# Computing the gating half v with seven products of block sums instead of eight of blocks

## The chip, the cores and the metric

One NeuronCore of a Trainium2 chip runs the whole program. Five engines work side by side, each through its own queue of instructions in a fixed order: TensorE (PE, matrix products, its weight loads listed as PEld), VectorE (DVE), ScalarE (ACT), GpSimd (POOL) and SyncE (SP, which here only issues DMAs). An instruction whose inputs are not there holds up all that is queued behind it on its engine. The metric is the device time of one execution in microseconds (us): less is better.

## The reference, cut to what matters

Two layers of a diffusion backbone over 512 latent tokens of 1024 features. Layer 0 is a neighbourhood attention followed by a squared-ReLU MLP, layer 1 a spatial gating unit followed by another MLP. The change is in the spatial gating unit, whose input h is 512 x 1024 and whose weight w_in is 1024 x 6144:

```
z = gelu(h @ w_in + b_in)
u, v = split(z, 2)
v = layer_norm(v, ln_g, ln_b)
s = einsum('gpq,bnqgc->bnpgc', w_s, v) + b_s
return (u * s) @ w_o
```

So v, before its norm, is gelu of a 512 x 1024 by 1024 x 3072 product and a bias. All is float32.

## The kernel before, in words

**Products.** A float32 value is split into two parts, hi (rounded to the TensorE format float32r) and lo (the rest), and a product is three matmuls, hi*hi, hi*lo and lo*hi (`products`, L178). Activations are split once per stage: `h_hi`/`h_lo` are eight tiles of 128 features x 512 tokens. Weights are split as they arrive.

**The weight stream.** All weights lie in one array in the order of their use (`SECTIONS`, L39), cut into units of 128 x 1536. `Weights.load` fetches a unit to a tile `raw` (768 KB, two buffers) through SP's queue. `Weights.upto` splits it in four pieces of 128 x 384: ACT casts `whi<-raw` (L80), DVE subtracts `wlo<-raw,whi` (L81). `get` asks for the pieces of one product and splits one unit ahead of them; three pairs whi/wlo, four after the attention, take turns.

**The stage of v** (L601 to L618). For each of six column blocks of 512 and each of four token blocks of 128, 24 matmuls of 512 columns (8 feature chunks by 3) fill one bank: 6 x 4 x 24 = 576 matmuls. Then DVE adds the bias (L616), ACT applies gelu (L617) and DVE takes the statistics of the later norm (L618). Behind it come the products of u (`u0`, ...), the norm of v and the products with w_s.

**The stage ahead of it** is the first MLP (`mlp`, L598): in two halves, 16 hidden blocks (24 matmuls each) and then 8 output blocks (48 matmuls each, L512 adds them to the residual stream `xall`). Into it 56 calls of `ada_block` are woven (L273): each loads 512 KB of the modulation weights to the one buffer `adaraw` (L276, SP) and reduces them on DVE (L277), so a load waits for the reduction before it. After the last output block `normed` (L494) makes the next `h_hi`/`h_lo`, token half by token half.

**The order.** Instructions are put into each engine's queue by a scheduler that works before the launch from its own estimates of times; the queues are then fixed. `tc.issue_after` binds an `ada_block` behind the hidden block that it follows, no more.

Of the kernel before, what the change touches and what calls it, by code (L numbers as in the profile page):

```python
# [10 lines left out]
F32 = mybir.dt.float32  # L11
F32R = mybir.dt.float32r
AF = mybir.ActivationFunctionType
ALU = mybir.AluOpType
# [3 lines left out]
P = 128  # L18
D = 1024
KC = D // P  # L20
T = 512
# [6 lines left out]
UNIT = 1536  # L28
# [9 lines left out]
# The weight stream: sections of pieces in the order of their use, (name, pieces, columns of a piece).  # L38
# [8 lines left out]

class Weights:
    """Streams of stationary or moving weight pieces, split into two float32r parts on arrival."""

    def __init__(self, nc, raw_pool, pool, wall, ahead=2):
        self.nc, self.raw_pool, self.pool, self.ahead, self.wall = nc, raw_pool, pool, ahead, wall
        self.first, self.width = {}, {}
        c = 0
        for key, n, w in SECTIONS:
            self.first[key], self.width[key] = c, w
            c += n * w
        self.tiles = {}
        self.raw = {}
        self.loaded = self.done = 0  # L60
        self.more, self.parts = None, 4

    def load(self, unit):
        while self.loaded <= min(unit, self.wall.shape[0] - 1):
            raw = self.raw_pool.tile([P, UNIT], F32, tag="raw", bufs=2, name="raw")
            self.nc.sync.dma_start(out=raw, in_=self.wall[self.loaded])
            self.raw[self.loaded] = raw
            self.loaded += 1

    def upto(self, unit):  # L70
        nc = self.nc
        while self.done <= min(unit, self.wall.shape[0] - 1):
            self.load(self.done)
            raw = self.raw.pop(self.done)
            pool = self.more if self.more is not None and self.done % 4 == 3 else self.pool
            hi = pool.tile([P, UNIT], F32R, tag="whi", name="whi")
            lo = pool.tile([P, UNIT], F32R, tag="wlo", name="wlo")
            for c in range(0, UNIT, UNIT // self.parts):
                cs = slice(c, c + UNIT // self.parts)
                nc.scalar.copy(out=hi[:, cs], in_=raw[:, cs])  # L80
                nc.vector.tensor_tensor(out=lo[:, cs], in0=raw[:, cs], in1=hi[:, cs], op=ALU.subtract)  # L81
            self.tiles[self.done] = (hi, lo)
            self.done += 1

    def get(self, key, i):
        w = self.width[key]
        u, c = divmod(self.first[key] + i * w, UNIT)
        assert c + w <= UNIT
        self.upto(u + self.ahead - 1)
        hi, lo = self.tiles[u]  # L90
        return hi[:, c:c + w], lo[:, c:c + w]
# [3 lines left out]
def backbone_kernel(ctx: ExitStack, tc: tile.TileContext, x0T, xT, cols, ada0, ada1, qknorm, bias_t,  # L95
                    wall, wsT, bs, binv, lngb, out):
    nc = tc.nc
# [10 lines left out]
    def mm():  # L108
        return bank("mm", 3)
# [16 lines left out]
    def mcol(l, v, kc):  # L126
        i = (l * 6 + v) * KC + kc
        return mod[:, i:i + 1]
# [5 lines left out]
    h_hi = [hp.tile([P, T], F32R, tag=f"hh{k}", name=f"hh{k}") for k in range(KC)]  # L134
    h_lo = [hp.tile([P, T], F32R, tag=f"hl{k}", name=f"hl{k}") for k in range(KC)]

    class Norm:
        """Reciprocal RMS over the feature axis (partitions and chunks), on every partition."""
# [39 lines left out]
    def products(o, terms, start, stop):  # L178
        n = len(terms) * 3
        i = 0  # L180
        for (ah, al), (bh, bl) in terms:
            for a, b in ((ah, bh), (ah, bl), (al, bh)):
                pe.matmul(o, lhsT=a, rhs=b, start=start and i == 0, stop=stop and i == n - 1)  # L183
                i += 1

# [297 lines left out]
    W.more = ctx.enter_context(tc.tile_pool(name="wb", bufs=1, reuse_waits="tile"))  # L483
# [15 lines left out]
    def normed(nm, A, shift):  # L499
        """What turns a finished half of the residual stream into the next sub-layer's input."""  # L500
        def go(c0, c1):
            r = nm.finish(c0, c1)
            modulated(xp, x, r, c0, c1, A, shift, h_hi, h_lo)
# [43 lines left out]
    nm = Norm(xp)  # L547
    residual("o", NPAIR, oh, ol, lambda m: mcol(0, 2, m), first=4, tail=3, nm=nm,
             then=normed(nm, A2[0], lambda k: mcol(0, 3, k)))
    ap_stack.close()  # L550

# [45 lines left out]
    nm = Norm(xp)  # L597
    mlp(0, "a", 24, 80, nm, normed(nm, A1[1], lambda k: mcol(1, 0, k)), None)  # L598
    cb_pool.close()

# [1 line left out]
    with tc.tile_pool(name="sg", bufs=1, reuse_waits="tile") as sp:  # L602
# [4 lines left out]
        for b in range(6):  # L607
            w = [W.get("v", b * KC + k) for k in range(KC)]
            bb = sp.tile([P, 512], F32, tag="bc", bufs=2, name="bc")
            act.dma_start(out=bb, in_=binv[b].partition_broadcast(P))  # L610
            for n in range(4):
                ns = slice(n * P, (n + 1) * P)
                o = mm()
                products(o, [((h_hi[k][:, ns], h_lo[k][:, ns]), w[k]) for k in range(KC)], True, True)
                vs = v[:, n, b * 512:(b + 1) * 512]
                vec.tensor_tensor(out=vs, in0=o, in1=bb, op=ALU.add)  # L616
                act.activation(out=vs, in_=vs, func=AF.Gelu)  # L617
                vec.bn_stats(out=stats[n][:, b], in_=vs)  # L618
# [19 lines left out]
        nm = Norm(xp)  # L638
        for part in range(4):
            gh, gl = [], []  # L640
            for i in range(6):
# [13 lines left out]
                for n in range(4):  # L655
# [15 lines left out]
                     then=normed(nm, A2[1], lambda k: mcol(1, 3, k)) if fin else None)  # L671

    mlp(1, "b", 80, 80, None, None, out)

# [102 lines left out]
```

## Time and profile before

| what | value |
|---|---|
| device time, median of 3 runs | 1563.95 us (1559.7 to 1568.19) |
| span of the profiled execution, first to last instruction (the only time shown of it) | 1560.2 us |
| PE busy | 1524.9 us, 98% of the span |
| DVE busy | 930.1 us, 60% |
| ACT busy | 664.3 us, 43% |
| stage of v on PE | 782.4 to 914.7 us |
| first MLP's second half, hidden blocks done on PE | 686.8 us |

Busy times of PE overlap, since matmuls are pipelined: the pitch from one start to the next is what a matmul costs. The same holds in part for DVE, where a run of instructions on independent data starts the next before the last is wholly written; the pitch is again read from starts. "Idle before" and the name behind an arrow tell how long an engine waited and for what.

### The profile page before, as it was taken

The page shows a single profiled execution, that of the slowest core. Times are in us where ns is not written, and L with a number is a line of the kernel's source. Part 1 is how long each engine was busy: PE and PEld are TensorE (multiplying, and loading weights), DVE is VectorE, ACT ScalarE, POOL GpSimd, SP SyncE. Part 2 cuts the span into 40 slices and gives each one's busy share as a digit, 9 for nine tenths or more (in the row PEclk, how much of TensorE's full clock was granted, in tenths as well). Part 3 has the DMA queues.
Part 4 walks back from the last instruction along what each step waited for, and adds up shares of the span by engine and source line. Part 5 has one row for each costly group of instructions (what it writes and reads, how often), then busy time and mean ns, then how long its engine had stood idle before and what let it go on. Part 6 is the DMA issues. An engine that isn't in the chain of part 4 may idle for free.

```text
span 1560.2 us, 21105 instructions
## 1 busy us (share of the span) xinstructions
PE 1524.9 (98%) x7780; PEld 1287.6 (83%) x7780; DVE 930.1 (60%) x1938; ACT 664.3 (43%) x1577; POOL 148.8 (10%) x177
## 2 busy tenths in 40 slices
PE   8899999999999999999999999999999999999999
PEld 2798888887898888878988887888889988888888
DVE  5778777777776555765575468644446743334431
ACT  2566666676544322442353256423234542224320
POOL 0522222212200000000100013100001000000000
PEclk9999999999999999999999999999999999999999
DMA  9265555535146555655243225322321432223230
GB/s 354 95 171 174 164 163 167 167 113 167 62 142 211 193 193 180 202 199 179 95 128 131 91 96 176 125 92 97 106 95 41 135 109 87 96 101 102 97 112 28
DMA packets 60311, 212.06 MB, mean 136 GB/s; under 512 B 7984, under 2 KB 16816, under 8 KB 58672
## 3 DMA queue, kind: packets, MB, share of 16 engines
q1 hardware_dynamic: 48688, 200.57, 39.2%
q10 hardware_dynamic: 11520, 10.15, 2.1%
q8 instruction: 61, 1.00, 0.3%
q14 instruction: 42, 0.34, 0.1%
HBM read 193.91 MB, written 2.10 MB: 126 GB/s over the span
## 4 chain that ended last, share of the span: by engine, by line
PE 59%; DMA 8%; DVE 4%; issue 2%; ACT 1%; ACTq 0%; DVEq 0%
PE ps_mm L183 29%; PE ps_t L183 19%; PE ps_o L183 9%; DMA adaraw<-ada 8%; DVE adaraw L277 1%; PE ps_s L656 1%; DVE wlo L81 1%; DVE nt L172 1%; DVE hl L174 0%; DVE xall L512 0%; DMA raw<-wall 0%; PE ps_s L156 0%; ACT v L632 0%; DVE acc L151 0%; ACT whi L80 0%
## 5 line engine op out<-in xcount | busy, mean ns | idle before, releaser
L80 ACT CAST whi<-raw 128x384 fp32r<-128x384 f32 x620 | 278.5, 510 | 355.9 <-PE ps_mm L183 141.5
L81 DVE TENSOR_TENSOR wlo<-raw,whi 128x384 fp32r<-128x384 f32 x620 | 330.6, 581 | 144.8 <-ACT whi L80 144.6
L277 DVE CUSTOM_DVE_ANT_0 adaraw<-adaraw,cb 128x1024 f32<-128x1024 f32 x80 | 99.4, 1242 | 106.6 <-DMA adaraw<-ada 106.1
L183 PE MATMUL ps_mm<-hh,wlo 128*128 128x512 f32 (+1 forms) x416 | 154.2, 371 | 0.6 <-DVE wlo L81 0.6
L183 PE MATMUL ps_mm<-hh,whi 128*128 128x512 f32 (+1 forms) x416 | 154.4, 371 | 0.0
L183 PE MATMUL ps_mm<-hl,whi 128*128 128x512 f32 (+1 forms) x416 | 154.0, 370 | 0.0
L183 PE MATMUL ps_mm<-whi,hh 128*128 128x384 f32 (+1 forms) x352 | 124.7, 356 | 5.1 <-DVE vl L332 2.9
L183 PE MATMUL ps_mm<-wlo,hh 128*128 128x384 f32 (+1 forms) x352 | 124.8, 355 | 1.9 <-DVE wlo L81 1.9
L183 PE MATMUL ps_mm<-mh,whi 128*128 128x512 f32 (+1 forms) x336 | 122.0, 363 | 3.2 <-ACT mh L566 3.2
L183 PE MATMUL ps_mm<-whi,hl 128*128 128x384 f32 (+1 forms) x352 | 124.1, 354 | 0.0
L183 PE MATMUL ps_mm<-ml,whi 128*128 128x512 f32 (+1 forms) x336 | 122.1, 363 | 0.0
L183 PE MATMUL ps_mm<-mh,wlo 128*128 128x512 f32 (+1 forms) x336 | 121.6, 362 | 0.0
L183 PE MATMUL ps_t<-hh,whi 128*128 128x512 f32 (+1 forms) x280 | 104.5, 373 | 0.0
L183 PE MATMUL ps_t<-hl,whi 128*128 128x512 f32 (+1 forms) x280 | 104.3, 372 | 0.0
L183 PE MATMUL ps_t<-hh,wlo 128*128 128x512 f32 (+1 forms) x280 | 104.0, 371 | 0.0
L183 PEld LDWEIGHTS ps_mm<-hh,wlo 128*128 128x128 f32 x416 | 78.5, 189 | 13.8 <-DVE wlo L81 0.8
L183 PEld LDWEIGHTS ps_mm<-hh,whi 128*128 128x128 f32 x416 | 78.5, 189 | 12.6
L183 PEld LDWEIGHTS ps_mm<-hl,whi 128*128 128x128 f32 x416 | 78.6, 189 | 12.5
L566 ACT CAST mh<-relu 128x512 fp32r<-128x512 f32 x64 | 39.7, 621 | 99.0 <-DVE relu L563 99.0
L183 PEld LDWEIGHTS ps_mm<-mh,whi 128*128 128x128 f32 x336 | 64.2, 191 | 13.1 <-ACT mh L566 3.6
L183 PEld LDWEIGHTS ps_mm<-whi,hh 128*128 128x128 f32 x352 | 66.6, 189 | 10.2 <-DVE vl L332 3.2
L183 PEld LDWEIGHTS ps_mm<-wlo,hh 128*128 128x128 f32 x352 | 66.8, 190 | 7.5 <-DVE wlo L81 2.8
(204 smaller groups left out, 3322.5 us busy)
## 6 DMA issues: line engine op xcount, KB each, us to landing
raw<-wall SPq DMA_DIRECT2D x155, 768.0 KB, 4.4
adaraw<-ada SPq DMA_DIRECT2D x80, 512.0 KB, 3.9
bt<-bias_t SPq DMA_DIRECT2D x16, 512.0 KB, 3.6
aw<-ada SPq DMA_DIRECT2D x7, 1024.0 KB, 10.8
q<-th SPq DMA_DIRECT2D x32, 128.0 KB, 2.4
q<-tl SPq DMA_DIRECT2D x32, 128.0 KB, 2.3
x<-x0T SPq DMA_DIRECT2D x3, 1024.0 KB, 11.3
bc<-lngb ACTq DMA_DIRECT2D x12, 256.0 KB, 3.3
```

The source lines that it names most:

```text
L80: nc.scalar.copy(out=hi[:, cs], in_=raw[:, cs])
L81: nc.vector.tensor_tensor(out=lo[:, cs], in0=raw[:, cs], in1=hi[:, cs], op=ALU.subtract)
L172: vec.scalar_tensor_tensor(out=t, in0=xk, scalar=A[:, k:k + 1], in1=r, op0=ALU.mult, op1=ALU.mult)
L183: pe.matmul(o, lhsT=a, rhs=b, start=start and i == 0, stop=stop and i == n - 1)
L277: vec.tensor_tensor_reduce(out=a, in0=a, in1=cb, scale=1.0, scalar=0.0, op0=ALU.mult, op1=ALU.add, accum_out=mod[:, idx:idx + 1])
L566: act.copy(out=a, in_=r)
L656: pe.matmul(s[:, n * P:(n + 1) * P], lhsT=v[:, n, g * P:(g + 1) * P], rhs=ws, start=True, stop=True)
```

## The change: what it does

The product for v is taken in three rounds, one for each 1024 columns of the weight. In a round h is cut into quarters (two halves of the features, B11 and B21 for the first 256 tokens, B12 and B22 for the last), the weight into four blocks W00, W10, W01, W11 of 512 features x 512 columns. Instead of eight block products the kernel forms seven (Winograd's form of Strassen's scheme): n1 = W00 with B11, n2 = W10 with B21, and five with sums T1 to T4 of quarters of h or with sums of weight blocks. Each is 4 feature chunks x 2 token blocks x 3 = 24 matmuls of 512 columns; three rounds have 3 x 7 x 24 = 504.

The sums of h are made once, ahead of the rounds: DVE adds hi and lo of each quarter again (4 instructions of 128 x 1024), forms T1, T3, T2 and T4 (4) and their lo parts (4), ACT casts their hi parts. The sums of weight blocks are made in every round on DVE from loads of the blocks: W01+W11 (kept in `sum0`, `sum1`, one for each half block), that plus W00, W00+W01 (in a raw tile), and the kept sum plus W10. The seven weight operands are then split like other weights. Bank X collects n1, n6, n7 and n4 without being cleared between, Z collects n5 and n3; after each product DVE takes what the bank holds so far into v, adding or subtracting, and gelu and statistics follow when a part is complete.

For this the weight stream is now loaded in tiles of 128 x 1024 (512 KB, three buffers) and split in pieces of 128 x 512 in the whole program; the eight tiles of `h_hi` and `h_lo` are one tile each; and the fourth pair of whi/wlo is given up during the stage of v and opened anew after it.

```diff
+PRODUCTS = (("n1", "B11"), ("n2", "B21"), ("n5", "T1"), ("n6", "T2"), ("n7", "T3"), ("n3", "B22"), ("n4", "T4"))
+def summands(blocks):
+    w00, w01, w10, w11 = blocks
+    return ((False, (w00,)), (False, (w10,)), (None, (w01, w11)), (True, (w00,)), (False, (w00, w01)),
+            (True, (w10,)), (False, (w11,)))
...
+            slot, go_on, what = self.stretches[self.loaded]
+            if go_on:
+                raw = self.sums[slot]
+            elif slot is None:
+                raw = self.raw_pool.tile([P, RAW], F32, tag="raw", bufs=3, name="raw")
+            else:
+                raw = self.sums[slot] = self.sum_pool.tile([P, RAW], F32, tag=f"sum{slot}", name=f"sum{slot}")
+            if not go_on:
+                self.nc.sync.dma_start(out=raw, in_=self.dram(what[0], RAW))
+                what = what[1:]
+            for c in what:
+                t = self.raw_pool.tile([P, RAW], F32, tag="raw", bufs=3, name="raw")
+                self.nc.sync.dma_start(out=t, in_=self.dram(c, RAW))
+                self.nc.vector.tensor_tensor(out=raw, in0=raw, in1=t, op=ALU.add)
...
+    def split(self, src, hi, lo):
+        self.nc.scalar.copy(out=hi, in_=src)
+        self.nc.vector.tensor_tensor(out=lo, in0=src, in1=hi, op=ALU.subtract)
...
-        for b in range(6):
-            w = [W.get("v", b * KC + k) for k in range(KC)]
...
-                products(o, [((h_hi[k][:, ns], h_lo[k][:, ns]), w[k]) for k in range(KC)], True, True)
...
+            for q, (ks, ts) in quarter.items():
+                f[q] = vp.tile([P, HK, HT], F32, tag="f" + q, name="f" + q)
+                vec.tensor_tensor(out=f[q], in0=hh_all[:, ks, ts], in1=hl_all[:, ks, ts], op=ALU.add)
+            def operand(name, a, b, reverse, into):
+                if reverse:
+                    vec.scalar_tensor_tensor(out=into, in0=a, scalar=-1.0, in1=b, op0=ALU.mult, op1=ALU.subtract)
+                else:
+                    vec.tensor_tensor(out=into, in0=a, in1=b, op=ALU.subtract)
...
+                act.copy(out=hi, in_=into)
+                vec.tensor_tensor(out=lo, in0=into, in1=hi, op=ALU.subtract)
...
+            for u in range(3):
...
+                into = {"n1": X, "n2": Y, "n5": Z, "n6": X, "n7": X, "n3": Z, "n4": X}
+                for j, (name, q) in enumerate(PRODUCTS):
+                    hi, lo = ops[q]
+                    o = into[name]
+                    for k in range(HK):
+                        w = W.get("v", (u * 7 + j) * HK + k)
+                        for i in range(2):
+                            ts = slice(i * P, (i + 1) * P)
+                            products(o[i], [((hi[:, k, ts], lo[:, k, ts]), w)],
...
+                        if name == "n6":
+                            plus(at_(1, 0), bb[:, 0])
+                        if name == "n7":
+                            minus(at_(1, 1), at_(1, 1))
+                            done = [(1, 1)]
+                        if name == "n3":
+                            plus(at_(1, 0), at_(1, 0))
+                            done = [(1, 0)]
```

DVE's queue where the stage of v begins, in the kernel before (the numbers behind hl and hh are the feature chunks' tiles):

```order
L159 RECIPROCAL rstd<-rstd 128x256
L81 TENSOR_TENSOR wlo<-raw,whi 128x384
L172 SCALAR_TENSOR_TENSOR nt<-xall,A_1_83,rstd 128x256 x2
L616 TENSOR_TENSOR v<-ps_mm,bc 128x512
L174 SCALAR_TENSOR_TENSOR hl_95<-nt,mod,hh_87 128x256
L170 TENSOR_TENSOR hl_96<-nt,hh_88 128x256
```

The same place in the changed kernel, from the last of the four sums of hi and lo on, which stand right behind the second token half's norm (fB are the quarters, sum_7827 is `sum0`):

```order
L683 TENSOR_TENSOR fB_7760<-hh,hl 128x1024
L690 TENSOR_TENSOR fB_7754<-fB_7754,fB_7756 128x1024
L115 TENSOR_TENSOR sum_7827<-sum_7827,raw 128x1024
L690 TENSOR_TENSOR fB_7756<-fB_7760,fB_7756 128x1024
L694 TENSOR_TENSOR T1l<-fB_7754,T1h 128x1024
L688 SCALAR_TENSOR_TENSOR fB_7760<-fB_7754,fB_7760 128x1024
L694 TENSOR_TENSOR T3l<-fB_7756,T3h 128x1024
L688 SCALAR_TENSOR_TENSOR fB_7758<-fB_7760,fB_7758 128x1024
L694 TENSOR_TENSOR T2l<-fB_7760,T2h 128x1024
L126 TENSOR_TENSOR wlo<-sum_7827,whi 128x512
L694 TENSOR_TENSOR T4l<-fB_7758,T4h 128x1024
```

The sums of h now stand as one block behind the norm, and the first split that n5 needs (`wlo<-sum_7827`) stands behind nearly all of it.

DVE's queue in the middle of the stage, before (raw_7998, raw_8124 and raw_8136 are units of the weight stream):

```order
L616 TENSOR_TENSOR v_7817<-ps_mm_8068,bc_8010 128x512
L81 TENSOR_TENSOR wlo_8001<-raw_7998,whi_8000 128x384 x4
L618 BN_STATS st2_7820<-v_7817 128x6
L81 TENSOR_TENSOR wlo_8127<-raw_8124,whi_8126 128x384 x4
L616 TENSOR_TENSOR v_7817<-ps_t_8096,bc_8010 128x512
```

And in the changed kernel's second round, where W00+W01 is formed (raw_8246 and raw_8277 are the two halves of W00, raw_8248 and raw_8279 those of W01, raw_8306 and raw_8315 those of W10):

```order
L115 TENSOR_TENSOR raw_8246<-raw_8246,raw_8248 128x1024
L126 TENSOR_TENSOR wlo_8241<-sum1_8177,whi_8240 128x512 x2
L126 TENSOR_TENSOR wlo_8241<-raw_8246,whi_8240 128x512
L728 SCALAR_TENSOR_TENSOR v_7744<-ps_s_8122,bb_8115 128x512
L728 SCALAR_TENSOR_TENSOR v_7744<-ps_s_8123,bb_8115 128x512
L126 TENSOR_TENSOR wlo_8274<-raw_8246,whi_8273 128x512
L731 TENSOR_TENSOR v_7744<-ps_mm_8118,bb_8115 128x512
L115 TENSOR_TENSOR raw_8277<-raw_8277,raw_8279 128x1024
L731 TENSOR_TENSOR v_7744<-ps_mm_8119,bb_8115 128x512
L126 TENSOR_TENSOR wlo_8274<-raw_8277,whi_8273 128x512 x2
L115 TENSOR_TENSOR sum0_8166<-sum0_8166,raw_8306 128x1024
L115 TENSOR_TENSOR sum1_8177<-sum1_8177,raw_8315 128x1024
```

Sums of freshly loaded tiles now stand between the splits and the steps that empty the banks, and an addition stands one row behind the last split of the tile three loads earlier.

DVE's queue in the first MLP, the last two hidden blocks of the second half, before:

```order
L563 SCALAR_TENSOR_TENSOR relu<-ps_t,relu 128x512
L567 TENSOR_TENSOR ml_7039<-relu,mh_7038 128x512
L81 TENSOR_TENSOR wlo<-raw,whi 128x384 x4
L277 ISA adaraw,mod<-adaraw,cb 128x1024
L277 ISA mod 128x1
L563 SCALAR_TENSOR_TENSOR relu<-ps_o,relu 128x512
L567 TENSOR_TENSOR ml_7083<-relu,mh_7082 128x512
```

And in the changed kernel:

```order
L628 SCALAR_TENSOR_TENSOR relu<-ps_t,relu 128x512
L336 ISA adaraw,mod<-adaraw,cb 128x1024
L336 ISA mod 128x1
L632 TENSOR_TENSOR ml_6974<-relu,mh_6973 128x512
L126 TENSOR_TENSOR wlo<-raw,whi 128x512 x3
L336 ISA adaraw,mod<-adaraw,cb 128x1024
L336 ISA mod 128x1
L628 SCALAR_TENSOR_TENSOR relu<-ps_o,relu 128x512
L632 TENSOR_TENSOR ml_7018<-relu,mh_7017 128x512
```

The change's text leaves this place alone, but the scheduler gave it another order: two reductions stand between the last two blocks where one stood. Counted over the queue, 56 of the program's 80 reductions stand ahead of the first of these 16 blocks in either kernel; ahead of the last block it was 71, and is 74. In the first half 37 stood ahead of the last hidden block, and 38 do now.

## Rows read from the trace of the kernel before

**Rows 1.** The page's first part: busy time, share and instructions of each engine.

```profile
PE 1524.9 (98%) x7780; PEld 1287.6 (83%) x7780; DVE 930.1 (60%) x1938; ACT 664.3 (43%) x1577; POOL 148.8 (10%) x177
```

**Rows 2.** Stretches: length, busy of PE, PEld, DVE, ACT, POOL, PEclk, DMA, GB/s.

```profile
782.40:914.70 132.30, 131.30 (x581) 108.45 (x580) 73.76 (x136) 50.60 (x105) 2.84 (x4) 1.00 0.34 112
```

**Rows 3.** PE in order of time, the stage of v: start, duration, instruction.

```profile
782.37 0.40 PE L183 MATMUL ps_mm<-whi,hh 128*128 128x512 f32 x1
...
786.50 0.70 PE L156 MATMUL ps_s<-acc,ones 128*128 128x256 f32 x2 [1.00 <-DVE acc L151]
...
914.47 0.39 PE L183 MATMUL ps_mm<-whi,hl 128*128 128x512 f32 x1
914.69 0.39 PE L183 MATMUL ps_mm<-hh,whi 128*128 128x512 f32 x1
```

**Rows 4.** DVE's groups in that stage: shapes, count, busy, mean ns, idle before.

```profile
L81 DVE TENSOR_TENSOR wlo<-raw,whi 128x384 fp32r<-128x384 f32 x67 | 33.0, 549 | 6.2 <-ACT whi L80 6.0
L618 DVE BATCH_NORM_STATS2 st<-v 128x6 f32<-128x512 f32 x23 | 15.9, 692 | 11.9 <-ACT v L617 11.9
```

**Rows 5.** DVE in order of time, the end of the second half's norm.

```profile
791.17 0.68 DVE L616 TENSOR_TENSOR v<-ps_mm,bc 128x512 f32<-128x512 f32 x1
791.77 0.47 DVE L174 SCALAR_TENSOR_TENSOR hl<-nt,mod,hh 128x256 fp32r<-128x256 f32 x1
...
794.28 0.69 DVE L618 BATCH_NORM_STATS2 st<-v 128x6 f32<-128x512 f32 x1
794.89 0.47 DVE L174 SCALAR_TENSOR_TENSOR hl<-nt,mod,hh 128x256 fp32r<-128x256 f32 x1
...
798.76 0.42 DVE L170 TENSOR_TENSOR hl<-nt,hh 128x256 fp32r<-128x256 f32 x1
```

**Rows 6.** DVE in order of time, the end of the stage of v.

```profile
912.14 3.30 DVE L81 TENSOR_TENSOR wlo<-raw,whi 128x384 fp32r<-128x384 f32 x7
...
922.40 1.23 DVE L635 TENSOR_TENSOR v<-v,bc 128x1024 f32<-128x1024 f32 x1
923.55 1.22 DVE L634 TENSOR_TENSOR v<-v,bc 128x1024 f32<-128x1024 f32 x1
```

**Rows 7.** DMA issues: tile, queue, count, size, median us to landing.

```profile
raw<-wall SPq DMA_DIRECT2D x155, 768.0 KB, 4.4
adaraw<-ada SPq DMA_DIRECT2D x80, 512.0 KB, 3.9
```

**Rows 8.** DVE in order of time, hidden blocks of the second half.

```profile
615.19 1.23 DVE L277 CUSTOM_DVE_ANT_0 adaraw<-adaraw,cb 128x1024 f32<-128x1024 f32 x1 [1.85 <-DMA adaraw<-ada]
...
621.59 1.23 DVE L277 CUSTOM_DVE_ANT_0 adaraw<-adaraw,cb 128x1024 f32<-128x1024 f32 x1 [3.19 <-DMA adaraw<-ada]
...
626.26 1.23 DVE L277 CUSTOM_DVE_ANT_0 adaraw<-adaraw,cb 128x1024 f32<-128x1024 f32 x1 [0.36 <-DMA adaraw<-ada]
...
632.12 1.23 DVE L277 CUSTOM_DVE_ANT_0 adaraw<-adaraw,cb 128x1024 f32<-128x1024 f32 x1 [0.77 <-DMA adaraw<-ada]
...
697.76 1.22 DVE L277 CUSTOM_DVE_ANT_0 adaraw<-adaraw,cb 128x1024 f32<-128x1024 f32 x1 [0.64 <-DMA adaraw<-ada]
698.91 0.68 DVE L563 SCALAR_TENSOR_TENSOR relu<-ps_o,relu 128x512 f32<-128x512 f32 x1
```

**Rows 9.** PE in order of time, the MLP's output blocks of each half.

```profile
512.69 0.39 PE L183 MATMUL ps_mm<-mh,whi 128*128 128x512 f32 x1
...
686.77 0.39 PE L183 MATMUL ps_mm<-mh,whi 128*128 128x512 f32 x1
...
700.30 0.80 PE L183 MATMUL ps_mm<-mh,whi 128*128 128x512 f32 x1 [3.17 <-ACT mh L566]
```

**Rows 10.** ACT in order of time, the first half's last hidden block.

```profile
517.88 0.62 ACT L566 CAST mh<-relu 128x512 fp32r<-128x512 f32 x1 [2.98 <-DVE relu L563]
```

**Rows 11.** Stretches behind PE's wait, columns as in Rows 2.

```profile
700.00:706.00 6.00, 5.70 (x13) 4.20 (x14) 3.19 (x8) 1.90 (x5) 0.00 (x0) 0.50 0.42 131
706.00:710.00 4.00, 4.00 (x18) 3.27 (x17) 2.42 (x5) 0.00 (x0) 0.00 (x0) 0.93 0.86 276
```

More of the change, by code (lines that the diff above doesn't have):

```diff
@@ L53, in __init__ @@
         self.first, self.width = {}, {}
+        self.stretches = []
         c = 0
         for key, n, w in SECTIONS:
-            self.first[key], self.width[key] = c, w
+            self.first[key], self.width[key] = len(self.stretches) * RAW, w
+            if key == "v":
+                for u in range(n // 16):
+                    at = c + 16 * u * w
+                    blocks = [at, at + 8 * w, at + 4 * w, at + 12 * w]
+                    for go_on, what in summands(blocks):
+                        for h in range(2):
+                            slot = None if go_on is False else h
+                            self.stretches.append((slot, go_on, [b + h * RAW for b in what]))
+            else:
+                assert n * w % RAW == 0
+                self.stretches += [(None, False, [b]) for b in range(c, c + n * w, RAW)]
@@ L57, in __init__, with dram @@
             c += n * w
-        self.tiles = {}
-        self.raw = {}
+        self.raw, self.tiles, self.sums = {}, {}, {}
         self.loaded = self.done = 0
[L61 to L66, printed above, removed]
+        self.more = self.sum_pool = None
+    def dram(self, c, n):
+        u, c = divmod(c, UNIT)
+        assert c + n <= UNIT
+        return self.wall[u][:, c:c + n]
@@ new lines, in load @@
+    def load(self, part):
+        last = min(part * PART // RAW, len(self.stretches) - 1)
+        while self.loaded <= last:
+            slot, go_on, what = self.stretches[self.loaded]
[12 more added lines that the diff above has]
+                self.nc.vector.tensor_tensor(out=raw, in0=raw, in1=t, op=ALU.add)
@@ L67, in load, with pair @@
             self.raw[self.loaded] = raw
             self.loaded += 1
-    def upto(self, unit):
-        nc = self.nc
-        while self.done <= min(unit, self.wall.shape[0] - 1):
-            self.load(self.done)
[L74 to L82, printed above, removed]
+    def pair(self, n):
+        pool = self.more if self.more is not None and n % 4 == 3 else self.pool
+        return (pool.tile([P, HILO], F32R, tag="whi", name="whi"),
+                pool.tile([P, HILO], F32R, tag="wlo", name="wlo"))
@@ new lines, in split, with upto @@
+    def split(self, src, hi, lo):
+        self.nc.scalar.copy(out=hi, in_=src)
+        self.nc.vector.tensor_tensor(out=lo, in0=src, in1=hi, op=ALU.subtract)
+    def upto(self, part):
+        while self.done <= min(part, len(self.stretches) * RAW // PART - 1):
+            self.load(self.done)
+            t, c = divmod(self.done * PART, HILO)
+            if t not in self.tiles:
+                self.tiles[t] = self.pair(t)
+            hi, lo = self.tiles[t]
+            r, rc = divmod(self.done * PART, RAW)
+            self.split(self.raw[r][:, rc:rc + PART], hi[:, c:c + PART], lo[:, c:c + PART])
@@ L83, in upto @@
             self.done += 1
+            if self.done * PART % RAW == 0:
+                del self.raw[r]
     def get(self, key, i):
         w = self.width[key]
[L87 to L90, printed above, removed]
+        t, c = divmod(self.first[key] + i * w, HILO)
+        assert c + w <= HILO
+        self.upto((t + self.ahead) * (HILO // PART) - 1)
+        hi, lo = self.tiles[t]
         return hi[:, c:c + w], lo[:, c:c + w]
@@ L132, in mvec @@
         return mod[:, i:i + KC]
-    h_hi = [hp.tile([P, T], F32R, tag=f"hh{k}", name=f"hh{k}") for k in range(KC)]
-    h_lo = [hp.tile([P, T], F32R, tag=f"hl{k}", name=f"hl{k}") for k in range(KC)]
+    hh_all = hp.tile([P, KC, T], F32R, name="hh")
+    hl_all = hp.tile([P, KC, T], F32R, name="hl")
+    h_hi = [hh_all[:, k] for k in range(KC)]
+    h_lo = [hl_all[:, k] for k in range(KC)]
     class Norm:
@@ L182, in products @@
             for a, b in ((ah, bh), (ah, bl), (al, bh)):
-                pe.matmul(o, lhsT=a, rhs=b, start=start and i == 0, stop=stop and i == n - 1)
+                pe.matmul(o, lhsT=a, rhs=b, start=start and i == 0, stop=stop and i == n - 1,
+                          skip_group_check=shared)
                 i += 1
```

86 lines of the change are left out of this document (69 added, 17 removed).

## The prediction

> **What bounds the kernel now.** I read the busy shares first: PE is busy for 98% of the span, DVE for 60% [rows 1], so over the whole program PE's matmuls are the bound. The share is a mean over stages, so I then took the stage of v by itself. From its first matmul at 782.37 to the first one of u at 914.69 [rows 3] there lie 576 matmuls of 512 columns and one wait of 1.0 us with two small matmuls (some 0.4 us): (132.3 - 1.4) / 576 = 0.227 us each. The clock is full there, and DVE is busy for 73.8 of 132.3 us, a little over half [rows 2]; among its groups the splits wlo and the statistics come first, and what it waited for was casts and gelu, not loads [rows 4]. So the stage is PE's, and DVE has about 58 us to spare. The question is what the change asks of DVE, and where.
>
> The third view is the order of time in the MLP ahead of it. There DVE waits again and again for `adaraw` [rows 8]: its queue holds one reduction between two hidden blocks, and a cycle of load and reduction takes as long as a hidden block on PE (24 x 0.227 = 5.45 us). PE's only wait of the second half follows from it: 3.17 us for the last hidden block's cast [rows 9]. This chain is just barely hidden before, and the change reorders it.
>
> **What the change takes away.** 576 - 504 = 72 matmuls of 0.227 us: 16.4 us of PE. It comes back as time only where PE sets the end, so I count DVE's side of the new stage.
>
> **DVE's work in the new stage.** Pitches, from start to start: 1.15 us for 128 x 1024, 3.30 / 7 = 0.47 us for a split of 384 columns [rows 6], 0.60 us for emptying a bank of 512 columns and 0.61 for statistics [rows 5]. Per column that is (1.15 - 0.60) / 512 = 1.07 ns, so a split of 512 columns takes 0.47 + 128 x 1.07 ns = 0.61 us. Counted in the changed queue from the first sum of hi and lo to the last bank emptied:
> - 36 of 128 x 1024 (12 for the operands T, 24 sums of weights): 36 x 1.15 = 41.4 us
> - 79 splits x 0.61 = 48.2 us
> - 42 banks emptied and 22 statistics, 64 x 0.60 = 38.4 us
>
> Together 128.0 us, against 16.4 us less on PE. One round alone has 8 sums, 28 splits, 14 banks and 8 statistics: 9.2 + 17.1 + 13.2 = 39.5 us on DVE, against 168 x 0.227 = 38.1 on PE. So DVE would be the bound by a little even if nothing ever waited.
>
> It also starts late. The four sums of hi and lo stand behind the second token half's norm, which ends at 798.76 + 0.42 = 799.2 now [rows 5]; in between stand two banks emptied and two statistics that the change moves away (one of each in the rows), 4 x 0.60, which leaves 796.8. PE does n1 and n2 from 782.4 meanwhile (48 matmuls, 10.9 us) and then has nothing: the first lo part that n5 needs is split behind twelve instructions of 1024 columns, 13.8 us after 796.8. Had DVE no wait at all, the stage would end at 796.8 + 128.0 = 924.8 instead of 914.7: 10.1 us later. The last matmuls lie beside the last rows of DVE's queue, within about 1 us.
>
> **The new waits for loads.** Sixteen raw tiles of a round take turns in three buffers, so the fourth load waits for the last reader of the first. For W00+W01 these are W00's and W01's first halves, then W00's second half, and W01's second half takes the buffer of the first sum, free only when that is split. In DVE's queue one bank is emptied between that split and the addition that needs the load. A like round trip is in the trace: from a reduction's end to the next reduction's start, with SP's issue and 512 KB between, 622.82 to 626.26 = 3.44 us with no other load beside it, and 627.49 to 632.12 = 4.63 with a load of 768 KB beside it [rows 7, 8]. The new loads come in twos of 512 KB; I take 4.1. The first wait is 4.1 - 0.60 = 3.5 us. The second half of W10 follows in the same manner behind the second sum's splits, with an addition of 1.15 and in two rounds of three a bank between: 4.1 - 1.15 - 0.4 = 2.55 us. So 6.05 us a round, 18.2 in three. Queued behind each on DVE are the splits for n3 and n4 and the emptying of X, for which PE waits. Bounds: 0 if other rows of the queue already run late enough to cover the loads, 7.1 a round by 4.63. The stage then ends at 943.0: **+28.3 us** (10 to 31).
>
> **The first MLP's order.** Ahead of the last hidden block of the second half DVE's queue holds 74 reductions instead of 71, both counted from 56 ahead of the first: 18 cycles instead of 15. The 15 took 697.76 - 615.19 = 82.6 us, 5.50 each [rows 8]; single ones took 4.67 without and 5.86 with a weight load beside. The loads are smaller now but come 16 times instead of 11 in this stretch, so I take 5.4: 18 x 5.4 = 97.2, and the last block's relu comes 14.6 us later. Behind it on DVE are that block's lo part and all later splits; PE waits for it with the 46th matmul of the output blocks. The 3.17 us become 17.8: **+14.6 us** (84.1 to 105.5 us of cycles: +1.5 to +22.9). In the first half one reduction more stands there. PE starts its output blocks at 512.69 and needs the last hidden part after 45 x 0.227 us, at 522.9; its cast ended at 518.50 [rows 9, 10]. A cycle of 5.4 more uses up the 4.4 us of slack: **+1 us** (0 to 1.5).
>
> **Edits taken at little or nothing.** Outside v 556 splits of 384 columns become 417 of 512: 261 to 254 us on DVE, as much on ACT, hidden behind PE; without cover a gain or a loss of 3 us. Casts, gelu and the table's load on ACT: 36 casts of 512 columns more, still well under DVE's time. The fourth whi/wlo pair given up in v: DVE is late there, not the pairs. Behind v the next statistics and norm have 49 matmuls (11.1 us) of u as cover, enough for the about 10 us that they take; without it, 2 us. The waits of PE lower its clock: behind the wait of 3.17 us the granted clock was 0.50, the lower of its levels (1.2 GHz), for the next 6 us and full soon after [rows 9, 11]. In the new stage such a slow start is mostly hidden, since DVE is later than PE: **+2 us**.
>
> **Sum.** 28.3 + 14.6 + 1 + 2 = 45.9 us on the profiled span of 1560.2: 1606.1. The median of the runs lies 3.75 us above that span; kept, that gives 1609.9.
>
> **Rivals.**
> 1. *The MLP's order costs nothing*: loads a third smaller bring a cycle to 4.67 throughout, and only v is slower. For it: DVE idled for the loads, not for work. Against: every load still waits for the one buffer's last reduction. 1563.95 + 28.3 + 2 = 1594.
> 2. *The loads in v come in time*, since DVE's rows there wait for PE as well and the two overlap: 10.1 instead of 28.3, 1592. Against: the three buffers' turn is fixed, whatever is late.
> 3. *PE's clock becomes the bound of v.* PE waits over 3 us about seven times there (once for T1 and about twice a round around n7); if every one costs 6.3 us at 0.50 as in [rows 11], 3.2 us each, and DVE then waits for the bank in turn, 7 x 3.2 = 22 us instead of the 2 taken: 1630. Against: the round leaves PE 7 us of slack. The Trainium skill, in TensorE: Matmul & The Clock Gate, section on HAM oscillation, says that a kernel whose bursts of matmuls are parted by waits for loads starts every burst at the low clock; the trace agrees in the one place where it has such a wait, and no run here yet shows a stage full of them.
> 4. *Faster: PE stays the bound.* DVE's queue keeps ahead, and the 16.4 us come out: 1547.6. It needs DVE's 128.0 us to fit into 914.7 - 16.4 - 796.8 = 101.5, that is pitches at 0.79 of the measured ones and no wait for loads; from there PE decides. For it: in the stage before, DVE was idle for 44%. Against: every row of 512 columns in it has the same pitch.
>
> **How the numbers follow.** Forecast 0.53 (1600 to 1622 by itself); rival 1 0.16, rival 2 0.11, rival 3 0.11, rival 4 0.05; 0.04 for rivals 1 and 2 together, 1576. The time is the forecast's, 1610. The range of 8 in 10, 1580 to 1628, reaches over rivals 1 and 2 and most of the way to 3. About 0.5% is what a measurement tells from no change (1556 to 1572): faster 0.05 by rival 4, the same 0.03 between that and rivals 1 and 2, slower 0.92.
>
> **What would show it.** Right: in the stage of v PE's share falls to about 0.7 and DVE's rises to 0.8 or more; PE waits for a split of `sum0` at n5 by 12 us or more; DVE waits some 3 us in each round at the additions, with the DMA named; the stage lasts about 160 us; PE's wait for the last hidden cast in the first MLP is about 18 us. Wrong: a stage of v under 135 us; DVE without waits for DMA at its additions; that cast's wait still near 3 us; a granted clock near 0.5 over large parts of v, which is rival 3.

## The result, and the profile after

The changed kernel takes 1608.9 us (median of 4 runs, 1604.9 to 1615.4), the kernel before beside it 1564.2. The ratio is 1.0276, 95% interval 1.023 to 1.0321: slower by 44.7 us, against 45.9 forecast. The time was right; where it comes from was right in part.

The lengths below run from the first matmul of a stage to the first of the next, read from PE in order of time in three profiles (the third is the kernel before once more, an experiment below). In the profiled runs the difference is 47.6 us.

| stage (us) | before | after | difference | before, second profile |
|---|---|---|---|---|
| up to the attention's output blocks | 390.0 | 399.9 | +9.9 | 395.1 |
| those blocks, norm, first hidden blocks | 122.7 | 121.4 | -1.3 | 122.6 |
| first MLP, output blocks of half 0 | 87.0 | 87.9 | +0.9 | 87.0 |
| hidden blocks of half 1 | 87.0 | 87.0 | 0 | 87.0 |
| output blocks of half 1 | 95.6 | 102.7 | +7.1 | 91.8 |
| v | 132.3 | 157.6 | +25.3 | 132.3 |
| u to the end | 645.5 | 651.3 | +5.8 | 645.8 |

The page's first part, which answers to [rows 1]: PE has fewer matmuls and a smaller share, DVE more work.

```profile
PE 1531.4 (95%) x7708; PEld 1281.1 (80%) x7708; DVE 987.0 (61%) x1872; ACT 674.6 (42%) x1461; POOL 148.9 (9%) x177
```

The stage of v by its three rounds and as a whole, columns as in [rows 2], to which the last row answers:

```profile
798.90:866.60 67.70, 46.61 (x173) 33.04 (x172) 59.70 (x83) 29.35 (x51) 2.65 (x4) 0.85 0.44 145
866.60:911.00 44.40, 40.82 (x170) 30.76 (x169) 39.21 (x58) 19.33 (x34) 0.00 (x0) 1.00 0.71 224
911.00:956.50 45.50, 40.94 (x169) 30.75 (x168) 39.44 (x58) 21.49 (x38) 0.00 (x0) 1.00 0.61 198
798.90:956.50 157.60, 128.37 (x508) 94.54 (x507) 138.35 (x198) 70.17 (x123) 2.65 (x4) 0.94 0.56 183
```

DVE is busy for 138.4 of 157.6 us, where it was 73.8 of 132.3. The second and third round have DVE full but for 5 or 6 us; the first is 23 us longer than these. Its reason stands in PE's order of time, the answer to [rows 3]:

```profile
798.93 0.40 PE L241 MATMUL ps_mm<-whi,hh 128*128 128x512 f32 x1
...
821.37 1.22 PE L241 MATMUL ps_s<-whi,T1h 128*128 128x512 f32 x2 [9.46 <-ACT whi L125]
828.14 0.79 PE L241 MATMUL ps_s<-wlo,T1h 128*128 128x512 f32 x1 [5.54 <-DVE wlo L126]
...
956.51 0.39 PE L241 MATMUL ps_mm<-hh,whi 128*128 128x512 f32 x1
```

and in DVE's, the answer to [rows 5]:

```profile
813.44 0.42 DVE L228 TENSOR_TENSOR hl<-nt,hh 128x256 fp32r<-128x256 f32 x1
813.78 4.62 DVE L683 TENSOR_TENSOR fB<-hh,hl 128x1024 f32<-128x1024 f32 x4
...
827.40 0.68 DVE L126 TENSOR_TENSOR wlo<-sum,whi 128x512 fp32r<-128x512 f32 x1
828.00 1.22 DVE L694 TENSOR_TENSOR T4l<-fB,T4h 128x1024 fp32r<-128x1024 f32 x1
```

PE ends n1 and n2 and waits 9.46 and 5.54 us, until DVE has ended the norm (813.8) and got through twelve instructions of 1024 columns and the first split of a sum (828.1). What DVE waited for from there to the last bank emptied (columns: us in all, times, longest):

```profile
DVE sum L115 <- DMA raw<-wall: 4.3, 5, 1.8
DVE wlo L126 <- ACT whi L125: 3.9, 5, 1.2
DVE st L754 <- ACT v L753: 3.4, 3, 2.2
DVE raw L115 <- DMA raw<-wall: 3.2, 3, 1.3
```

That is 7.5 us for loads at the additions, 7.3 for casts and gelu.

PE at the output blocks of the MLP's second half has four waits where [rows 9] has one of 3.17 us; below them two reductions, as in [rows 8]: the last one ahead of the half's first hidden block (the 56th of the program) and the last one ahead of its last (the 74th):

```profile
707.27 0.50 PE L241 MATMUL ps_mm<-ml,whi 128*128 128x512 f32 x1 [1.85 <-DVE ml L632]
709.28 0.80 PE L241 MATMUL ps_mm<-mh,whi 128*128 128x512 f32 x1 [1.27 <-ACT mh L631]
712.00 0.80 PE L241 MATMUL ps_mm<-ml,whi 128*128 128x512 f32 x1 [1.93 <-DVE ml L632]
717.66 0.80 PE L241 MATMUL ps_mm<-mh,whi 128*128 128x512 f32 x1 [4.44 <-ACT mh L631]
```
```profile
622.12 1.23 DVE L336 CUSTOM_DVE_ANT_0 adaraw<-adaraw,cb 128x1024 f32<-128x1024 f32 x1 [1.94 <-DMA adaraw<-ada]
...
715.12 1.23 DVE L336 CUSTOM_DVE_ANT_0 adaraw<-adaraw,cb 128x1024 f32<-128x1024 f32 x1 [1.38 <-DMA adaraw<-ada]
```

Two places had not been forecast at all. In the attention, which works on one pair of heads after the other, ACT's queue now has a cast that waits for its weight load ahead of the softmax; PE's scores wait as long behind it, at five of the steps from pair to pair by 1.1 to 1.9 us (first ACT's waits of this kind from 85 to 385 us, with us in all, times and longest, and one of them; then PE):

```profile
ACT whi L125 <- DMA raw<-wall: 8.3, 5, 1.9
189.32 0.62 ACT L125 CAST whi<-raw 128x512 fp32r<-128x512 f32 x1 [1.87 <-DMA raw<-wall]
```
```profile
191.87 0.50 PE L460 MATMUL ps_s<-kk,q 128*128 128x512 f32 x1 [1.87 <-ACT pb L467]
```

And behind v PE waits for the layer norm and, longest, for the gates (`gh`):

```profile
967.93 1.13 PE L795 MATMUL ps_s<-ws,v 128*128 128x128 f32 x8 [0.60 <-DVE v L774]
...
1002.46 0.79 PE L241 MATMUL ps_mm<-gh,whi 128*128 128x512 f32 x1 [2.45 <-ACT gh L804]
```

### The profile page after: what moved, and what is told of

It is laid out like the page before. It is cut to its first block, busy times and chain, and to the rows that moved or that the text cites. A ratio compares the mean times of both kernels' runs of the same rounds, so it can differ in the third digit from the quotient of the medians.

```text
span 1607.8 us, 21067 instructions
## 1 busy us (share of the span) xinstructions
PE 1531.4 (95%) x7708; PEld 1281.1 (80%) x7708; DVE 987.0 (61%) x1872; ACT 674.6 (42%) x1461; POOL 148.9 (9%) x177
## 5 line engine op out<-in xcount | busy, mean ns | idle before, releaser
L125 ACT CAST whi<-raw 128x512 fp32r<-128x512 f32 x464 | 264.6, 619 | 393.2 <-PE ps_mm L241 138.4
L126 DVE TENSOR_TENSOR wlo<-raw,whi 128x512 fp32r<-128x512 f32 x464 | 318.9, 723 | 152.2 <-ACT whi L125 151.4
L241 PE MATMUL ps_mm<-whi,hh 128*128 128x384 f32 (+1 forms) x280 | 98.9, 354 | 6.2 <-DVE vl L391 2.9
L241 PE MATMUL ps_mm<-wlo,hh 128*128 128x384 f32 (+1 forms) x280 | 97.6, 349 | 0.2
L241 PE MATMUL ps_mm<-whi,hl 128*128 128x384 f32 (+1 forms) x280 | 97.4, 350 | 0.0
L241 PEld LDWEIGHTS ps_mm<-ml,whi 128*128 128x128 f32 x336 | 64.1, 191 | 15.7 <-DVE ml L632 6.1
L570 DVE SCALAR_TENSOR_TENSOR xall<-ps_mm,mod,xall 128x512 f32<-128x512 f32 (+1 forms) x47 | 30.7, 657 | 69.5 <-PE ps_mm L241 69.5
## 6 DMA issues: line engine op xcount, KB each, us to landing
q<-th SPq DMA_DIRECT2D x32, 128.0 KB, 2.4
q<-tl SPq DMA_DIRECT2D x32, 128.0 KB, 2.3
```

What stands on the lines that cost most here:

```text
L125: self.nc.scalar.copy(out=hi, in_=src)
L126: self.nc.vector.tensor_tensor(out=lo, in0=src, in1=hi, op=ALU.subtract)
L570: vec.scalar_tensor_tensor(out=x[m][:, c0:c1], in0=o[:, c0:c1], scalar=gate(m), in1=x[m][:, c0:c1], op0=ALU.mult, op1=ALU.add)
```

## The experiments

Ratios are to the kernel before on the same chip, with 95% intervals. Lengths of stages are from one profile each, read as in the table above.

**e1: eight products on the changed stream.**
```
-for u in range(3): ...               # rounds of seven products
+for b in range(6): ...               # as before; pieces of 1024, splits of 512 stay
```

> The changed kernel's weight stream (pieces of 1024 columns, splits of 512) with the eight products of the kernel before in the stage of v. Theory A (the profile after splits the 47.6 us by place: attention +8.6, first half of the first MLP +0.9, output blocks of its second half +7.1, v +25.3, behind v +5.8; the first three come from the smaller pieces, the rest from the seven products): 1564.2 + 16.6 = 1581, output blocks of the second half 102 to 103 us long, stage of v 132 to 135, behind v 645 to 647. Rival B (all of it follows from the products, and the attention's shift is chance): 1564. Rival C (the 5.8 behind v belong to the stream as well): 1587.

Measured: 1577.7 us, ratio 1.0081 (1.005 to 1.0112). Attention to 397.9, output blocks of the second half 99.2, v 133.3, u to the end 647.9. Theory A holds but for 3 us in the MLP: some 14 of the 44.7 us come from the stream, the other 31 from the seven products. Rival C's 1587 is missed. Of the 5.8 us behind v 2.4 belong to the stream and 3.4 to the products by these single profiles; the split is not firm, since e7, with stream and products as before, has 647.2 there.

**e2: seven products on the old stream.**
```
-UNIT = 2048            +UNIT = 3072
+  self.stretches.append((None, False, [flat], HILO, HILO // 4))    # outside v
```


> Seven products as in the changed kernel, but outside v the weights come as before, in pieces of 1536 columns split by 384; the raw buffers are one ring of 3072 columns, two pieces outside v and three inside. Order of reductions and hidden blocks in the MLP is again that of before. Theory A (the smaller pieces cost 16.6 us ahead of v): 1608.9 - 16.6 = 1592, attention and MLP as long as before (first output block of the second half at about 687 us), stage of v still about 158. Rival B (the shift in the attention comes from the single tile for the parts of h, which stays here, and only the MLP comes back): 1601. Rival C (all follows from the products): 1609.

Measured: 1601.4 us, 1.0233 (1.019 to 1.0276). The MLP is as before: half 0 87.0, output blocks of half 1 96.1. But v takes 164.0, and the attention still ends at 397.9, though none of the waits of 1.9 us is left. The number is rival B's; its reason, the one tile for the parts of h, can stand behind half of the 7.9 us at most (e11). Why the ring costs v 6 us, in its third round above all (50.6), is not settled: PE's queue also has matmuls of n3 and n4 in alternation here, where the changed kernel has one product behind the other.

**e3: the sums over 64 columns.**
```
-self.nc.vector.tensor_tensor(out=raw, in0=raw, in1=t, op=ALU.add)
+self.nc.vector.tensor_tensor(out=raw[:, :64], in0=raw[:, :64], in1=t[:, :64], op=ALU.add)
```

> The changed kernel with each of the 24 sums of weight blocks done over 64 of its 1024 columns; the rest of the sums is left out, loads, buffers and waits stay. Theory A (DVE sets the stage of v): 24 x (1.15 - 0.1) = 25 us of DVE's work go, PE then bounds: n5 starts at about 827 and 456 matmuls of 0.227 follow, 103.5 us, so the stage ends at 931 to 935 instead of 956.5: 1608.9 - 23 = 1586 (1583 to 1590), DVE's share in the stage from 0.89 to about 0.8. Rival B (the loads' round trip sets the stage): it loses at most what DVE gains between waits, the waits for loads grow from 7.5 to over 20 us, and the time stays at 1600 or above. Rival C (PE's clock sets it): 1600 or above with a granted clock under 0.9 over the stage.

Measured: 1593.9 us, 1.0189 (1.0151 to 1.0227); v 147.7. The three rounds:

```profile
799.10:858.10 59.00, 42.98 (x172) 33.07 (x171) 51.39 (x82) 28.04 (x49) 2.64 (x4) 0.86 0.50 166
858.10:906.90 48.80, 42.01 (x169) 33.38 (x168) 35.52 (x63) 23.53 (x41) 0.00 (x0) 0.93 0.70 220
906.90:946.80 39.90, 39.01 (x170) 31.39 (x169) 32.12 (x61) 20.65 (x35) 0.00 (x0) 1.00 0.68 222
```

Between both theories: 24 us less of DVE's work shorten v by 9.9. The start stays (PE waits 9.30 and 4.74 us). In the second round DVE is busy for 35.5 us and the round still takes 48.8: waits for loads rise from 7.5 to 11.7 us, those for casts from 3.9 to 11.1. The edit also moved PE's queue: in the second round one matmul of n3 stands ahead of all of n7 and waits 4.03 us for its cast, with a granted clock of 0.50 for the 6.8 us behind it. So DVE's work alone doesn't set a round; that the loads hold it with three buffers is what e9 tests.

**e4: two buffers for the table's rows.**
```
-a = cbp.tile([P, D], F32, tag="adaraw", name="adaraw")
+a = (ada2[0] if i % 2 and ada2 else cbp).tile([P, D], F32, tag="adaraw", name="adaraw")
+ada2.append(normp)                   # ahead of the first MLP
```

> The changed kernel with two buffers for the table's rows in the first MLP instead of one, so that a load need not wait for the reduction before it; all reductions then stand ahead of the thirteenth hidden block of the second half. Theory A (the one buffer's cycle of about 5.2 us puts DVE behind PE in the second half): the waits of 9.5 us at its output blocks go, they last 92 to 93 us instead of 102.7, and the 0.9 of the first half goes too: 1608.9 - 10.5 = 1598 (1597 to 1601). Rival B (the loads together run at the limit of the DMA engines in the MLP, whatever the buffers): output blocks stay near 102 and the time at 1606 to 1609.

Measured: 1598.7 us, 1.0222 (1.0188 to 1.0257). The output blocks of the second half take 89.1 us instead of 102.7, without any wait for a hidden part: the single buffer is their cause. But in the first half they go from 87.9 to 93.5: reductions move there, and two waits of 1.20 and 1.80 us cost 6.5 us, since PE's clock falls behind them:

```profile
530.50:537.30 6.80, 5.52 (x13) 4.36 (x14) 3.31 (x7) 0.62 (x1) 0.00 (x0) 0.50 0.93 296
```

Theory A, with a price it did not name: more was gained in the second half than forecast, and lost again in the first, so that the total fits by luck.

**e5: the first round by eight products.**
```
-for u in range(3):
+plain()                       # blocks 0 and 1 as before, then the operands T
+for u in range(1, 3):
```


> The changed kernel with its first round of v by eight products, as before, and only the other two by seven; the operands T are built beside the first round's matmuls. In the changed kernel the three rounds take 67.7, 44.4 and 45.5 us on PE, the first with 15 us of waits before the first product of T. Theory A (the late start is the largest part of what v loses): the first round falls to 192 x 0.227 = 43.6 us and 2 for the norm, the other two keep 44 to 46 each, the stage is 135 us and the time 1608.9 - 22.6 = 1586. Rival B (DVE's total sets the stage wherever the operands are built): DVE's 128 us lose one round's sums and little else, some 12 us, and the stage ends no earlier than 813 + 118 + 16 of waits, 148 us in all: 1599.

Measured: 1583.4 us, 1.0132 (1.0102 to 1.0162); v 136.3. Theory A, to 1.3 us: the late start is the largest part of what v loses. PE reaches the first product of T at 853.3 and waits for nothing there.

**e6: the sums on GpSimd.**
```
-self.nc.vector.tensor_tensor(out=raw, in0=raw, in1=t, op=ALU.add)
+self.nc.gpsimd.tensor_tensor(out=raw, in0=raw, in1=t, op=ALU.add)
```

> The changed kernel with the 24 sums of weight blocks on GpSimd instead of VectorE, everything else alike. An addition of 1024 columns takes GpSimd 2.4 us in the layer norm of this program, 1.15 on VectorE. Theory A (DVE's work sets the second and third round): they fall from 44.4 and 45.5 to at most 41, the first keeps its start, the stage is 148 to 150 as in the run with sums of 64 columns: 1600. Rival B (the chain load, sum, cast, split of a piece sets them, and becomes 1.2 us longer with each sum): no gain or a loss, 1606 to 1618.

Measured: 1623.7 us, 1.0381 (1.035 to 1.0412); v 178.9. Slower still, beyond what rival B's chain gives. Groups in v (count | busy, mean ns | idle before):

```profile
L115 POOL TENSOR_TENSOR sum<-sum,raw 128x1024 f32<-128x1024 f32 x18 | 45.3, 2522 | 72.8 <-DMA raw<-wall 28.9 <-DVE st L754 22.9 <-DVE wlo L126 19.1
L126 DVE TENSOR_TENSOR wlo<-sum,whi 128x512 fp32r<-128x512 f32 x36 | 44.0, 1257 | 11.8 <-ACT whi L125 11.6
L126 DVE TENSOR_TENSOR wlo<-raw,whi 128x512 fp32r<-128x512 f32 x48 | 37.5, 809 | 16.2 <-ACT whi L125 16.2
```

In the changed kernel both kinds of split take 681 ns; here those of sums take 1257. The 61 splits that no addition overlaps take 0.69 us at most; 16 of the other 23 take 1.66 to 2.90. One of the longest starts 0.4 us after the start of an addition and ends 0.55 us after its end:

```profile
936.45 2.75 POOL L115 TENSOR_TENSOR sum<-sum,raw 128x1024 f32<-128x1024 f32 x1 [1.28 <-DVE wlo L126]
936.85 2.90 DVE L126 TENSOR_TENSOR wlo<-sum,whi 128x512 fp32r<-128x512 f32 x1
```

The Trainium skill, in SBUF — State Buffer, section "Who interferes with whom", says that a DVE instruction with two SBUF inputs contends with a GpSimd instruction that reads SBUF, for a port pair which it calls an exclusive lock. The trace agrees with these two rows. Of the 24 x 1.15 = 27.6 us taken off DVE, its 84 splits took back 44.0 + 37.5 - 84 x 0.68 = 24.4.

**e7: two buffers in the second half, on the kernel before.** The line of `adaraw` as in e4, and
```
+if half == 1 and l == 0: ada2.append(extra_ada)      # a pool of its own
```

> The kernel before with two buffers for the table's rows in the second half of the first MLP; nothing else changes. In the changed kernel two buffers cut the output blocks of this half from 102.7 to 89.1 us; before they took 95.6. Theory A (the one buffer's cycle costs the kernel before its wait of 3.17 us and the slow clock behind it): they take 89 to 90, and the time is 1563.7 - 6.5 = 1557 (1556 to 1560). Rival B (loads of both streams together delay the weights): the hidden blocks of that half get longer than 87.0 us, and the time stays within 1561 to 1566. Its attention, which is the same work in the same order as in the kernel before, also shows whether that stage's end at 390.0 us can be relied on.

Measured: 1565.8 us (10 runs, 1556.0 to 1569.8), 1.0006 (0.9983 to 1.0029). The profile has the 89.1 us of theory A, no wait, hidden blocks of 87.0 and a span of 1554.2; but it is the fastest of the ten runs, and the median shows no gain. What the slower runs spend the 6 us on no profile here shows; this stays open. e11 names one place where runs of one program differ by 3 us.

**e8: the edits of e5 and e7 together, on the changed kernel.**

> First round of v by eight products and two buffers for the table's rows in the second half of the first MLP together, on the changed kernel. If the two terms are independent, 22.6 us in v and 13.7 in the output blocks go: 1608.9 - 36.3 = 1573 (1570 to 1578). If the first round of v is also held by what the MLP's queue left late, the gain is smaller: 1580 to 1586. In neither is it faster than the kernel before.

Measured: 1575.9 us, 1.0078 (1.0054 to 1.0102). v 137.7, output blocks 90.8: the two terms add up to within 3 us.

**e9: e8 with seven raw buffers in the two rounds of seven products.**
```
+fp = tile_pool("fp")     # the sums of hi and lo; closed after operands()
+W.four = tile_pool("vr") # in their place four more raw pieces, used in turn with the three
```


> The kernel with one round of eight products and two buffers for the table's rows (1575.9 us), and in its two rounds of seven products seven raw buffers instead of three; the four more lie where the sums of hi and lo were, which are dead by then. Theory A (each of these rounds loses 2.5 us of DVE's time to loads that wait for a buffer, and some 2 us to casts behind them): they fall from about 45 to 41, the stage of v from 137.7 to 130, the waits of DVE for raw pieces to under 1 us a round, and the time to 1569. Rival B (DVE's 39.5 us of work and the order of its queue set a round): the waits for loads go but turn into others, and the stage stays within 2 us of 137.7: 1574 to 1577.

Measured: 1568.5 us, 1.003 (1.0004 to 1.0056); v 127.3, 5 us less than with eight products throughout. The profile is of the fastest of ten runs (1561.1). The rounds:

```profile
783.60:831.50 47.90, 45.09 (x196) 35.96 (x195) 40.88 (x59) 23.30 (x42) 2.61 (x4) 1.00 0.47 151
831.50:870.90 39.40, 38.54 (x169) 31.46 (x168) 39.18 (x59) 20.50 (x37) 0.00 (x0) 1.00 0.75 247
870.90:910.90 40.00, 38.60 (x169) 31.47 (x169) 39.77 (x61) 20.19 (x35) 0.00 (x0) 1.00 0.54 172
```

DVE is busy for 39.2 of 39.4 us and 39.8 of 40.0, with 0.4 us of waits in both. Theory A: the three buffers were behind the waits for loads and, at one remove, behind those for casts and gelu. In the same two rounds of e8 DVE waited 12.1 us: 4.1 for loads, 4.6 for casts and gelu and, once, 3.0 for the bias, which ACT's queue loads. DVE's queue there has the same order in both but for a few rows. What is left is DVE's own work.

**e10: e9 with the edit of e2.**

> The last kernel (one round of eight products, two buffers for the table's rows, seven raw buffers) with the weights outside v in pieces of 1536 columns split by 384, as before. If the stream's cost in the attention and in the first half of the MLP (some 9 us in the medians of the run with eight products on the changed stream) goes and the stage of v keeps what it has, it comes to 1557 to 1563, at or below the kernel before: a candidate that beats both. If the ring of raw buffers costs v again what it did with seven products throughout (164.0 against 157.6 us), 1563 to 1570.

Measured: 1569.5 us, 1.0045 (1.0024 to 1.0066). v keeps 128.0, so the ring costs nothing with seven buffers; the attention ends at 393.7, the output blocks of the first half take 87.0. But those of the second half take 96.2, with waits for hidden parts again, and u to the end 649.9, with three waits of 1.2 to 2.1 us at the layer norm and the gates. Not the candidate expected.

**e11: the kernel before, a second profile.**

> The kernel before, unchanged, for a second profile. Its runs lie between 1556 and 1571 us, more than those of most kernels on the changed stream, and its attention ended at 390.0 us in the first profile, at 388.9 in that with two buffers for the table's rows (which was the fastest of its ten runs), but at 397.9 where the old pieces came with seven products. Theory A (the attention of this order varies from run to run by what DVE and GpSimd happen to do at the same time): this profile has it end anywhere from 389 to 398, by as much as its time differs from the first. Rival B (390 is fixed, and the 397.9 came from the single tile for the parts of h): 389 to 391, whatever the time.

Measured: 1563.5 us, attention to 395.1, against 390.0: theory A. 3.0 of the 5.1 us arise at 58.7 us, in two scalings on DVE beside a row of memsets on GpSimd; first this profile's row, then the first profile's:

```profile
58.68 3.81 DVE L258 TENSOR_SCALAR h<-x,A1c,modc 128x256 f32<-128x256 f32 x2
```
```profile
58.89 0.81 DVE L258 TENSOR_SCALAR h<-x,A1c,modc 128x256 f32<-128x256 f32 x2
```

e2 and e12 have the same slow pair, no other profile has it. The same section of the Trainium skill lets a scaling in a mode that uses both ports wait for GpSimd; the trace agrees as far as the two fall together, but no row shows the mode, and no run here took the memsets away.

So the +9.9 of the table is no clean measure of the stream. Over the profiles the attention ends at 388.9 to 397.9 with the old stream (six) and at 394.3 to 400.4 with the new one (eight), 4.4 us apart in the mean. But the slow pair stands in three of the six, which end at 395.1 to 397.9; the other three end at 388.9 to 393.7, and from these the eight lie 7.3 us apart in the mean. All eight have the five waits of ACT's casts for loads, 8.1 to 9.0 us in all; none of the six has one.

e2's lateness has a second part. Set against the first profile score by score it is 3.7 us late at 331.5 and 7.8 at 384.6. Over the same last pair of heads e10 and e12 lose 3.3 us, the eight with the new stream 2.4 to 2.8, e7 and e11 nothing. All that lose there have the one tile for the parts of h; that it is the cause no run shows.

**e12: a candidate.** e10 with
```
-for u in range(1, 3):
+for u in range(1, 2):                # then plain() once more, for blocks 4 and 5
-a = (ada2[0] if i % 2 and ada2 else cbp).tile(...)
+a = (ada2[0] if i % 2 and i >= 48 else cbp).tile(...)
```

> The last kernel on the old stream, with only the middle round of v by seven products, the first and third by eight, and the second buffer for the table's rows from row 48 on, so that it opens in the output blocks of the MLP's first half, where DVE idles. Theory A (each cost has its own place): v 43.6 + 2 + 40 + 43.6 = 129 us, output blocks of the second half 89 to 90 instead of 96.2, and behind v no late norm, some 4 us less than the 649.9 of that run: 1569.5 - 7 - 4 + 1 = 1559, a little below the 1562.7 of the kernel before. Rival B (the waits come back elsewhere: the first half's output blocks over 90, or the first layer norm late all the same): 1563 to 1570, not below it.

Measured: 1561.9 us (12 runs), 0.9996 (0.9978 to 1.0013): the same as before. Output blocks of the second half 89.1 and u to the end 645.3, as theory A has it; v 131.5 instead of 129: the middle round takes 39.9, but the first 47.8 instead of 45.6. Its attention has the slow pair of e11 and ends at 397.1. No version here beats the kernel before by more than a measurement can tell.

## Why the prediction was right, and where not

- **DVE becomes the bound of v: right.** From the first sum to the last bank emptied DVE was busy for 128.6 us (128.0 forecast) in 144.9 (146.2). e9, where nothing else is left, has rounds of 39.4 and 40.0 against the 39.5 of work worked out.
- **The late start: right.** DVE began 14.9 us after v's first matmul (14.4), the first low part was ready 14.3 us later (13.8), PE waited 15.0 us (12 or more). e5 shows it by taking it away: 21.3 us less in v.
- **The waits for loads: right in sum, wrong in kind.** Of the 18.2 us forecast 16.2 came, only 7.5 of them named as loads. e9 shows that most others waited at one remove: e8's two rounds are 43.2 and 47.0, 10.8 us more than e9's 79.4, so 5.4 a round against 6.05. The two places reckoned, W01's and W10's second halves, do not make up that sum alone.
- **v in all: +25.3 against 28.3.** PE's share came out at 0.81, not 0.7: its rounds count as busy for 46.6, 40.8 and 40.9 us where pitches give 38.1, with the lower clock in the first alone. The clock cost more than the 2 us taken: in the first round 67.7 - 38.1 leaves 29.6 us, of which 21 are waits that PE's rows name; some 4 of the other 8 are matmuls at the lower clock (0.85 in the mean), the rest slow starts behind the waits. In the other rounds it is full, so rival 3 falls.
- **The MLP's order: right in mechanism, too large.** +7.1 (+11.0 against the second profile) for 14.6. The 18 cycles took 715.12 - 622.12 = 93.0 us, 5.17 each and not 5.4, which is 4.2 us less; and they began 13.0 us behind the half's first matmul where it had been 15.5, a shift of 2.5 us that the sum left out. So the last relu came 7.9 us later against PE, not 14.6, and PE had four waits of 9.5 us in all, not one of 17.8. e4 confirms the cause, so rival 1 falls.
- **Outside, 0 plus or minus 3: wrong.** The failing step is "hidden behind PE". ACT's casts are in its queue ahead of the softmax, and a cast that waits for a load holds the scores: 8.3 us of such waits, and 8.6 us between the two profiles with the attention's output blocks (e11 has the means of all). Behind v another 5.8, where 11.1 us of cover were counted against about 10 of work: waits of 3.7 us for the layer norm, the table w_s and the gates, and slow matmuls behind the last (a granted clock of 0.81 over the next 17.6 us). In the profiles these 14.4 us stand against 12.6 counted too much before (v 3.0, MLP 7.6, clock 2); the total came out right by luck, since they cancelled.
- **Rivals 2 and 4** fall: v took 157.6 us. What rival 4 would have needed e9 shows: loads in time, by seven buffers, and no late start; then v takes 127.3 against 132.3, and its rounds of seven are still DVE's.

## What to carry to other kernels

Fewer matmuls paid for with additions save nothing once the engine that adds is full: work out that engine's time for one round (39.5 us here) against PE's (38.1) and against what the round costs undone (43.6), with buffers enough that no load waits. Where the operands must be built first, start with a round that doesn't need them. And changing a weight stream's piece and split reorders every queue it passes through, so look for a waiting cast ahead of work that PE needs, also in stages that the change does not touch.

## What the runs showed of the hardware

Additions on GpSimd slow DVE's subtractions on other data: 1257 ns in the mean instead of 681 for those of sums, up to 2.90 us for one (e6). Two scalings on DVE took 3.81 us beside GpSimd's memsets and 0.81 in another run of the same program (e11). Short waits cost more than their length: in e4 3.0 us of waits made a stretch 6.5 us longer, with a granted clock of 0.50 (1.2 GHz) for 6.8 us and matmuls that last 0.63 us there instead of 0.39.
